# Other instruction prices in the list schedule of a hybrid decoder layer

## The chip, the core and the metric

The kernel runs as one program on one core of a Trainium2 chip. TensorE (PE in the profile; its weight loads are PEld) multiplies matrices into PSUM, VectorE (DVE) and ScalarE (ACT) do elementwise work, GpSimd (POOL) a little, and SyncE (SP) issues the DMAs. The metric is the time of one execution on the device in microseconds (us); less is better.

## What is computed

One layer of a decoder with two kinds of heads. 2128 tokens go through it: 16 meta tokens and 2048 prompt tokens as one sequence, and 8 sample sequences of 8 tokens each. The width is 1024. After an RMS norm one projection gives q, k, v and u:

```python
q, k, v, u = mixer_front(xp, g_mix, w_in, g_q, g_k)
o_att = prompt_window_attention(q, k, v, sinks)        # window 128, 8 query heads, 2 kv heads
o_ssm, hr, hi = ssm_mixer(u, h0, h0, *ssm_p)           # 32 groups, 64 complex states each
xp = mixer_back(xp, o_att, o_ssm, *back_p)

def mixer_back(x, o_att, o_ssm, g_att_out, g_ssm_out, w_out, g_ffn, w_gate, w_up, w_down):
    mix = concat([rms_norm(o_att, g_att_out), rms_norm(o_ssm, g_ssm_out)])
    h = x + mix @ w_out
    f = rms_norm(h, g_ffn)
    return h + (silu(f @ w_gate) * (f @ w_up)) @ w_down
```

The state mixer turns u into 64 complex states a group by a scan over the positions, h = lambda h + B u, reads them out with C, and ends with a GELU and a gate. All inputs and outputs are float32; the inner width of the FFN is 2816.

## The kernel before

**A recorder and a planner.** The kernel's stages don't issue instructions. Every call on an engine is recorded by `Plan.note` (line 225) with its dependencies (read after write, write after read and after write by regions of tiles, and reuse of a buffer), its cost from `Plan.price` (line 316) and its engine. The profile gives line 279, the call in `note`, for nearly all instructions. At the end `Plan.issue` (line 341) lays all recorded instructions in an order, once, by list scheduling: each has a tail, its cost plus the longest chain of costs behind it, with `hop` (line 296) added for each step between two instructions, and a bias for some parts (`BIAS`, line 288: attention 6 us, the state mixer's later steps more and more). The planner keeps a clock for each engine. It goes on with the engine that can start earliest, and there takes the one with the longest tail among those that are ready by then. The eight PSUM banks are given out in the same walk. The instructions are then issued in the order of their planned starts, each on its engine, SP's DMAs among them. So a price never changes an instruction; it changes the place of instructions in the queues of the engines, and which bank a product gets. An engine works its queue off in that order and stands when the next instruction's inputs aren't there.

**Prices before.** ns for n elements per partition: VectorE 1.04 n + 65 (0.52 n for copies and scalar operations from SBUF, 65 more for a scalar operand that is a tile), for the scan and the masked maximum too; ScalarE 0.83 n + 60 or 95, and 90 for each of bias, scale tile and accumulator; TensorE 0.417 n + 3 for products in fp32r, 1.68 n + 3 in fp32, 0.85 per row for a transpose.

**Stages** (by the names of `part`):
- `u` (`phase_u`, line 502): six blocks of tokens. A block's x is split in a high and a low part in fp32r (xh on ScalarE, xl on VectorE), three products per weight tile (`mm3`, line 433) add up pu in PSUM, 96 products of up to 384 columns a block; 1/rms comes from sums over partitions (pb) and a pow on GpSimd; VectorE writes us = pu x 1/rms through a view whose inner step isn't one element. Beside it `aw` splits the qkv weights.
- `prep` (`phase_prep`, line 570): the parameters of the state mixer, on VectorE mostly; they go through DRAM (kD, miD).
- `att` and `ssm` (`mix_step`, line 1201): 17 tiles of 128 tokens for attention and 16 blocks of two groups for the state mixer, recorded side by side. Attention of a tile: 48 products pa in fp32r (q, k, v), qn on VectorE, transposes pt, 16 score products on 64 rows in pairs for the two kv heads (`scores`, line 1032), masked maxima mx on VectorE, exp on ScalarE, transposes of P, then four products P x V with 64 output columns each, in pairs for the two kv heads (`p_v`, line 1099). The state mixer of two groups: product px, rotation on VectorE in products of 64 partitions (xt, xs), two scans (gg), rotation back, hc (`ssm_h`, line 883), product yp of hc (`ssm_y`, line 889), GELU on ScalarE and VectorE (g), gate product px, store to oD. Every second step also makes tables of sine and cosine (f, y, co, si).
- `ow`, `out`, `start`, `norm`, `turn`: output projection (products po), norms and operands of the FFN.
- `ffn` (`phase_ffn`, line 1428): the FFN by a scheme with seven products in place of eight (ga, gb, gc, da, db).

Of the kernel before, what the change touches and what calls it, by code (L numbers as in the profile page):

```python
# [9 lines left out]
F32R = mybir.dt.float32r  # L10
# [160 lines left out]

class Op:
    __slots__ = ("eng", "cost", "wait", "call", "deps", "order", "next", "succ", "tail", "left", "ready", "start", "n", "set", "tiles",
                 "into", "part", "dma", "port")


class Plan:
# [18 lines left out]
    def turn(self, old, *new):  # L196

        pools = [LazyPool(self, *p) for p in new]

        def call():  # L200
            for p in [p for p in reversed(self.open) if p in old]:
                p.ctx.close()
                self.open.remove(p)
            for p in pools:
                p.ctx = ExitStack()
                p.got = p.ctx.enter_context(self.tc.tile_pool(name=p.name, bufs=p.bufs, side=p.side))
                self.open.append(p)

        if not old:
            call()  # L210
            return pools
        g = Op()
        g.eng, g.n, g.cost, g.wait, g.set, g.tiles, g.into = "gate", len(self.ops), 0, 0, None, [], None
        g.part = None
        g.order, g.dma, g.port = set(), False, False
        g.deps = set().union(*[p.ops for p in old])
        for p in old:
            p.over = True
        for p in pools:
            p.gate = g.n  # L220
        g.call = call
        self.ops.append(g)
        return pools

    def note(self, eng, name, args, kw):
        o = Op()
# [7 lines left out]
        deps, order = set(), set()  # L234
# [31 lines left out]
        o.dma = "dma" in name  # L266
        o.cost, o.wait = self.price(eng, name, args, kw)
        o.port = self.ported(eng, name, outs, args, kw)
        fn = args[2] if eng == "scalar" and name == "activation" else None
        o.set = {AF.Sin: "sin", AF.Silu: "silu", AF.Exp: "exp", AF.Tanh: "exp"}.get(fn)  # L270

# [5 lines left out]
        def call():  # L277
# [9 lines left out]

    part, BIAS = None, {"prep": 3e3, "att": 6e3, **{"ssm%d" % i: 2e3 * (i - 4) for i in range(5, 17)}}

    HOP = {("tensor", "scalar"): 200, ("tensor", "vector"): 200, ("tensor", "gpsimd"): 225,  # L290
           ("vector", "tensor"): 256, ("vector", "scalar"): 200, ("vector", "gpsimd"): 205,
           ("scalar", "tensor"): 281, ("scalar", "vector"): 142, ("scalar", "gpsimd"): 170,
           ("gpsimd", "tensor"): 135, ("gpsimd", "vector"): 74, ("gpsimd", "scalar"): 75,
           ("tensor", "tensor"): 0, ("vector", "vector"): 127, ("scalar", "scalar"): 150, ("gpsimd", "gpsimd"): 102}

    def hop(self, a, b):
        if "gate" in (a, b):
# [3 lines left out]
        return 1100 if a == "sync" else self.HOP[a, b]  # L301

    PORT = False

    def ported(self, eng, name, outs, args, kw):

# [9 lines left out]
    def price(self, eng, name, args, kw):  # L316

        psum = lambda v: isinstance(v, Lazy) and v.base.psum
        out = kw.get("out", args[0] if args else None)
        n = int(np.prod(out.shape[1:]))  # L320
        ap = lambda v: isinstance(v, (Lazy, bass.AP))
        if "dma" in name:
            return 100 + out.shape[0] * n * 4 / (370 if out.shape[-1] >= 128 else 190), 1000
        if eng == "tensor":
            if name == "transpose":
                return 0.85 * args[1].shape[0], 0
            return (0.417 * n if args[1].dtype == F32R else 1.68 * max(n, 64)) + 3, 0
        if eng == "scalar":
            c = 0.83 * n + (60 if psum(args[1]) else 95) + 90 * ap(kw.get("bias")) + 90 * ap(kw.get("scale")) + 90 * ("accum_out" in kw)
            return c, 0  # L330
        if eng == "vector":
            if name == "tensor_reduce":
                return 1.04 * int(np.prod(args[1].shape[1:])) + 70, 0
            fast = name in ("tensor_copy", "tensor_scalar", "memset") and not psum(args[1] if len(args) > 1 else None)
            c = 65 + 65 * (name in ("tensor_scalar", "scalar_tensor_tensor") and ap(args[2]))
            return (3 if name == "reciprocal" else 0.52 if fast else 1.04) * n + c, 0
        if kw.get("op") == ALU.pow:
            return 165 * n + 300, 0
        return {"tensor_scalar": 1.37, "memset": 0.8, "tensor_copy": 1.0}.get(name, 2.15) * n + 135, 0

    def issue(self):
# [28 lines left out]
        banks = [(0.0, "b%d" % i) for i in range(8)]  # L370
        whole = {b: False for _, b in banks}
        left = {t: t.count for o in ops for t in o.tiles if t.psum}
        order, table, pipe, port = [], None, 0.0, 0.0
        for _ in ops:
            get = [min((b for b in banks if whole[b[1]] or not y), default=(1e12,)) for y in (False, True)]
            at = lambda o: (max(o.ready, get[o.into.seeded][0], 1e12 * bool(need.get(o.into))) if o.into and "tag" not in o.into.kw
# [3 lines left out]
            o = max((o for o in cand[e] if at(o) <= t), key=lambda o: o.tail)  # L380
# [10 lines left out]
            end = t + o.cost  # L391
            if o.dma:
                pipe = end = max(t + 2000 * (e == "gpsimd"), pipe) + o.cost
            if o.set is not None and o.set != table:
                end += 1283
                table = o.set
            free[e] = t + 1340 if o.dma and e == "gpsimd" else end
            if o.port:
                port = end
# [1378 lines left out]
```

## Time and profile before

| | |
|---|---|
| time, median of 3 runs | 2149.49 us (2148.3 to 2153.83) |
| profiled execution | 2150.36 us, of which its span 2148.5 us |
| TensorE busy | 2049.7 us (95%) |
| VectorE busy | 1735.1 us (81%) |
| ScalarE busy | 1295.8 us (60%) |
| mean granted clock of TensorE | 0.977 |

The span runs from the first to the last instruction. By the products in the trace the stage of u ends near 130 us, the mixers near 560, the output projection near 775, and the rest is the FFN. "Busy" is the union of an engine's instructions; a product in fp32 has two records, one in fp32r has one. The granted clock is 1.00 at 2.4 GHz; a mean below that over a stretch says that part of it ran at 1.2 GHz.

### The profile page before, as it was taken

The page shows a single profiled execution, that of the slowest core. Times are in us where ns is not written, and L with a number is a line of the kernel's source. Part 1 is how long each engine was busy: PE and PEld are TensorE (multiplying, and loading weights), DVE is VectorE, ACT ScalarE, POOL GpSimd, SP SyncE. Part 2 cuts the span into 40 slices and gives each one's busy share as a digit, 9 for nine tenths or more (in the row PEclk, how much of TensorE's full clock was granted, in tenths as well). Part 3 has the DMA queues.
Part 4 walks back from the last instruction along what each step waited for, and adds up shares of the span by engine and source line. Part 5 has one row for each costly group of instructions (what it writes and reads, how often), then busy time and mean ns, then how long its engine had stood idle before and what let it go on. Part 6 is the DMA issues. An engine that isn't in the chain of part 4 may idle for free.

```text
span 2148.5 us, 35113 instructions
## 1 busy us (share of the span) xinstructions
PE 2049.7 (95%) x12625; PEld 1938.0 (90%) x12625; DVE 1735.1 (81%) x3688; ACT 1295.8 (60%) x2831; POOL 101.6 (5%) x97
## 2 busy tenths in 40 slices
PE   7989988898999999999999999999999999999998
PEld 7977766665898999999999899999999999999997
DVE  8776999987488769878788888878877987877876
ACT  6335766657444437566566756656656775665665
POOL 2001120112011000000000000000000000000000
PEclk9899999998899999999999999999999999999999
DMA  6673332224343645323322553332322722222222
GB/s 224 151 145 77 80 86 74 69 73 126 93 122 90 181 150 176 104 76 112 105 80 79 174 160 103 116 94 81 115 70 99 243 87 89 79 69 88 81 70 87
DMA packets 195150, 235.05 MB, mean 109 GB/s; under 512 B 54000, under 2 KB 155792, under 8 KB 194832
## 3 DMA queue, kind: packets, MB, share of 16 engines
q1 hardware_dynamic: 194976, 232.81, 36.3%
q8 instruction: 99, 1.62, 0.3%
q14 instruction: 75, 0.61, 0.1%
HBM read 187.92 MB, written 45.83 MB: 109 GB/s over the span
## 4 chain that ended last, share of the span: by engine, by line
PE 77%; DVE 14%; ACT 4%; DMA 3%; issue 1%; POOL 1%; SPq 0%; DVEq 0%; ACTq 0%
PE ga L279 23%; PE gc L279 12%; PE db L279 11%; PE da L279 8%; PE po L279 7%; PE gb L279 6%; PE pa L279 3%; PE pu L279 2%; PE ps L279 2%; DVE xs L279 2%; DVE xt L279 1%; DVE P L279 1%; PE pt L279 1%; PE yp L279 1%; ACT wb L279 1%
## 5 line engine op out<-in xcount | busy, mean ns | idle before, releaser
L279 PE MATMUL ga<-X,wb 128*128 128x352 f32 x3168 | 721.0, 324 | 7.0 <-ACT acc L279 2.9
L279 PEld LDWEIGHTS ga<-X,wb 128*128 128x128 f32 x3168 | 544.0, 188 | 10.9 <-ACT gb L279 3.8
L279 PE MATMUL gc<-X,wb 128*128 128x352 f32 x1584 | 401.6, 323 | 2.4 <-ACT acc L279 1.4
L279 PEld LDWEIGHTS gc<-X,wb 128*128 128x128 f32 x1584 | 278.7, 188 | 3.6 <-ACT acc L279 2.3
L279 ACT ACTIVATE wb<-S 128x512 fp32r<-128x512 f32 (+1 forms) x306 | 187.4, 617 | 154.3 <-PE ga L279 74.3
L279 DVE TENSOR_TENSOR wb<-S,wb 128x512 fp32r<-128x512 f32 (+1 forms) x306 | 203.5, 670 | 57.9 <-ACT wb L279 26.7
L279 ACT ACTIVATE wb<-r 128x512 fp32r<-128x512 f32 (+1 forms) x242 | 146.9, 613 | 124.9 <-PE gc L279 46.2
L279 PE MATMUL gb<-X,wb 128*128 128x352 f32 x792 | 216.7, 323 | 0.0
L279 PE MATMUL da<-wb 128*128 128x352 f32 x936 | 208.9, 323 | 3.2 <-DVE acc L279 1.6
L279 DVE TENSOR_TENSOR wb<-r,wb 128x512 fp32r<-128x512 f32 (+1 forms) x242 | 159.9, 668 | 51.6 <-PE gb L279 22.3
L279 PE MATMUL db<-wb 128*128 128x352 f32 x792 | 162.9, 323 | 4.4 <-ACT db L279 4.4
L279 PEld LDWEIGHTS da<-wb 128*128 128x128 f32 x936 | 159.4, 188 | 5.5 <-ACT wb L279 4.6
L279 PE MATMUL db<-gb,wb 128*128 128x352 f32 x792 | 161.0, 323 | 0.0
L279 ACT ACTIVATE wb<-fr 128x512 fp32r<-128x512 f32 (+1 forms) x166 | 101.9, 619 | 92.0 <-PE gc L279 40.1
L279 PE MATMUL pa<-wb,xh 128*128 128x512 f32 (+3 forms) x544 | 143.8, 357 | 0.3 <-DVE qn L279 0.3
L279 DVE TENSOR_TENSOR wb<-fr,wb 128x512 fp32r<-128x512 f32 (+1 forms) x166 | 110.8, 674 | 39.3 <-PE gb L279 16.0
L279 PEld LDWEIGHTS gb<-X,wb 128*128 128x128 f32 x792 | 142.2, 188 | 0.0
L279 PEld LDWEIGHTS db<-wb 128*128 128x128 f32 x792 | 132.7, 188 | 6.0 <-ACT db L279 6.0
L279 PEld LDWEIGHTS db<-gb,wb 128*128 128x128 f32 x792 | 133.1, 188 | 0.3 <-ACT db L279 0.3
L279 ACT ACTIVATE acc<-db 128x352 f32<-128x352 f32 x288 | 119.5, 457 | 20.7 <-PE db L279 19.9
L279 PE MATMUL po<-oh,wb 128*128 128x352 f32 x576 | 121.8, 335 | 2.1 <-ACT oh L279 1.5
L279 ACT ACTIVATE db<-acc 128x352 f32<-128x352 f32 x276 | 120.5, 465 | 2.4 <-DVE ru L279 2.2
(257 smaller groups left out, 3746.8 us busy)
## 6 DMA issues: line engine op xcount, KB each, us to landing
r<-w_up SPq DMA_DIRECT2D x41, 512.0 KB
r<-w_gate SPq DMA_DIRECT2D x38, 512.0 KB
r<-w_down SPq DMA_DIRECT2D x34, 512.0 KB
fr<-w_gate SPq DMA_DIRECT2D x28, 512.0 KB
fr<-w_down SPq DMA_DIRECT2D x26, 512.0 KB
fr<-w_up SPq DMA_DIRECT2D x25, 512.0 KB
acc<-xT SPq DMA_DIRECT2D x6, 1408.0 KB
hD<-acc SPq DMA_DIRECT2D x6, 1408.0 KB
```

The source lines that it names most:

```text
L279: getattr(getattr(self.nc, eng), name)(*[f(v) for v in args], **{k: f(v) for k, v in kw.items()})
```

## The change

Three things change in the planner. The hops between engines get other values for six of the pairs. The price of an instruction depends on its part: for parts outside `DENSE` (the output projection, its weights, norms and the FFN) a product in fp32r costs 11 ns more, and elementwise operands whose innermost step isn't one element cost more per element. For all parts, 64-partition VectorE work costs 100 ns more, the scan 2.1 n + 60, the masked maximum 1.08 n + 75, VectorE's rate is 1.05 in place of 1.04, and products in fp32 cost half where they use 64 rows or 64 columns of the array, and 3 ns more of fixed cost. Last, the planner adds 95 ns after a product whose geometry (64 rows, 64 columns, full) differs from that of the product planned before it. No instruction is added, removed or changed; their order and the banks may change.

```diff
--- before.py
+++ after.py
@@ -171,7 +171,7 @@
 
 class Op:
     __slots__ = ("eng", "cost", "wait", "call", "deps", "order", "next", "succ", "tail", "left", "ready", "start", "n", "set", "tiles",
-                 "into", "part", "dma", "port")
+                 "into", "part", "dma", "port", "geo")
 
 
 class Plan:
@@ -212,7 +212,7 @@
         g = Op()
         g.eng, g.n, g.cost, g.wait, g.set, g.tiles, g.into = "gate", len(self.ops), 0, 0, None, [], None
         g.part = None
-        g.order, g.dma, g.port = set(), False, False
+        g.order, g.dma, g.port, g.geo = set(), False, False, None
         g.deps = set().union(*[p.ops for p in old])
         for p in old:
             p.over = True
@@ -266,6 +266,7 @@
         o.dma = "dma" in name
         o.cost, o.wait = self.price(eng, name, args, kw)
         o.port = self.ported(eng, name, outs, args, kw)
+        o.geo = self.geometry(args) if eng == "tensor" else None
         fn = args[2] if eng == "scalar" and name == "activation" else None
         o.set = {AF.Sin: "sin", AF.Silu: "silu", AF.Exp: "exp", AF.Tanh: "exp"}.get(fn)
 
@@ -287,11 +288,11 @@
 
     part, BIAS = None, {"prep": 3e3, "att": 6e3, **{"ssm%d" % i: 2e3 * (i - 4) for i in range(5, 17)}}
 
-    HOP = {("tensor", "scalar"): 200, ("tensor", "vector"): 200, ("tensor", "gpsimd"): 225,
-           ("vector", "tensor"): 256, ("vector", "scalar"): 200, ("vector", "gpsimd"): 205,
-           ("scalar", "tensor"): 281, ("scalar", "vector"): 142, ("scalar", "gpsimd"): 170,
+    HOP = {("tensor", "scalar"): 200, ("tensor", "vector"): 200, ("tensor", "gpsimd"): 275,
+           ("vector", "tensor"): 256, ("vector", "scalar"): 118, ("vector", "gpsimd"): 165,
+           ("scalar", "tensor"): 281, ("scalar", "vector"): 142, ("scalar", "gpsimd"): 180,
            ("gpsimd", "tensor"): 135, ("gpsimd", "vector"): 74, ("gpsimd", "scalar"): 75,
-           ("tensor", "tensor"): 0, ("vector", "vector"): 127, ("scalar", "scalar"): 150, ("gpsimd", "gpsimd"): 102}
+           ("tensor", "tensor"): 0, ("vector", "vector"): 119, ("scalar", "scalar"): 133, ("gpsimd", "gpsimd"): 102}
 
     def hop(self, a, b):
         if "gate" in (a, b):
@@ -301,6 +302,14 @@
         return 1100 if a == "sync" else self.HOP[a, b]
 
     PORT = False
+    DENSE = "out", "start", "norm", "turn", "ffn", "ow"
+
+    def geometry(self, args):
+
+        out, a = args[0], args[1]
+        rows = a.shape[0]
+        c = a.shape[1] if len(a.shape) > 1 else 1
+        return "rows" if rows == 64 else "cols" if out.shape[0] == 64 and c == 64 else "full"
 
     def ported(self, eng, name, outs, args, kw):
 
@@ -324,16 +333,25 @@
         if eng == "tensor":
             if name == "transpose":
                 return 0.85 * args[1].shape[0], 0
-            return (0.417 * n if args[1].dtype == F32R else 1.68 * max(n, 64)) + 3, 0
+            if args[1].dtype == F32R:
+                return 0.417 * n + (3 if self.part in self.DENSE else 14), 0
+            return 1.68 * max(n, 64) * (0.5 if self.geometry(args) != "full" else 1) + 6, 0
+
+        slow = self.part not in self.DENSE and sum(isinstance(v, Lazy) and v.shape[-1] > 1 and v.idx.strides[-1] not in (0, v.idx.itemsize)
+                   for v in list(args) + list(kw.values()))
         if eng == "scalar":
-            c = 0.83 * n + (60 if psum(args[1]) else 95) + 90 * ap(kw.get("bias")) + 90 * ap(kw.get("scale")) + 90 * ("accum_out" in kw)
+            c = (0.83 + 1.08 * bool(slow) * (name == "activation")) * n + (60 if psum(args[1]) else 95) + 90 * ap(kw.get("bias")) + 90 * ap(kw.get("scale")) + 90 * ("accum_out" in kw)
             return c, 0
         if eng == "vector":
             if name == "tensor_reduce":
                 return 1.04 * int(np.prod(args[1].shape[1:])) + 70, 0
             fast = name in ("tensor_copy", "tensor_scalar", "memset") and not psum(args[1] if len(args) > 1 else None)
-            c = 65 + 65 * (name in ("tensor_scalar", "scalar_tensor_tensor") and ap(args[2]))
-            return (3 if name == "reciprocal" else 0.52 if fast else 1.04) * n + c, 0
+            c = 65 + 100 * (out.shape[0] == 64) + 65 * (name in ("tensor_scalar", "scalar_tensor_tensor") and ap(args[2]))
+            if name == "tensor_tensor_scan":
+                return 2.1 * n + 60, 0
+            if name == "tensor_tensor_reduce":
+                return 1.08 * n + 75, 0
+            return ((3 if name == "reciprocal" else 0.52 if fast else 1.05) + 0.75 * (slow > 0)) * n + c, 0
         if kw.get("op") == ALU.pow:
             return 165 * n + 300, 0
         return {"tensor_scalar": 1.37, "memset": 0.8, "tensor_copy": 1.0}.get(name, 2.15) * n + 135, 0
@@ -370,7 +388,7 @@
         banks = [(0.0, "b%d" % i) for i in range(8)]
         whole = {b: False for _, b in banks}
         left = {t: t.count for o in ops for t in o.tiles if t.psum}
-        order, table, pipe, port = [], None, 0.0, 0.0
+        order, table, pipe, port, geo = [], None, 0.0, 0.0, None
         for _ in ops:
             get = [min((b for b in banks if whole[b[1]] or not y), default=(1e12,)) for y in (False, True)]
             at = lambda o: (max(o.ready, get[o.into.seeded][0], 1e12 * bool(need.get(o.into))) if o.into and "tag" not in o.into.kw
@@ -394,6 +412,9 @@
             if o.set is not None and o.set != table:
                 end += 1283
                 table = o.set
+            if o.geo != geo and o.geo:
+                end += 95
+                geo = o.geo
             free[e] = t + 1340 if o.dma and e == "gpsimd" else end
             if o.port:
                 port = end
```

## Rows read from the trace of the kernel before

**Rows 1.** The page: busy us of each engine, its share of the span, and instructions.
```profile
PE 2049.7 (95%) x12625; PEld 1938.0 (90%) x12625; DVE 1735.1 (81%) x3688; ACT 1295.8 (60%) x2831; POOL 101.6 (5%) x97
```

**Rows 2.** Busy us by stage: stretch, length, engines, then PEclk, DMA share, GB/s.
```profile
0.00:130.00 130.00, 115.33 (x668) 111.47 (x669) 105.47 (x270) 63.08 (x110) 17.68 (x12) 0.91 0.69 188
130.00:170.00 40.00, 31.07 (x168) 26.98 (x166) 33.55 (x67) 13.44 (x18) 5.06 (x6) 0.88 0.68 131
170.00:240.00 70.00, 68.89 (x483) 54.14 (x483) 45.55 (x163) 48.22 (x127) 8.91 (x11) 0.99 0.27 68
240.00:450.00 210.00, 186.62 (x1060) 136.84 (x1060) 198.39 (x526) 139.21 (x321) 32.12 (x39) 0.97 0.29 80
450.00:510.00 60.00, 55.22 (x318) 39.88 (x316) 46.96 (x140) 28.10 (x82) 7.18 (x7) 0.97 0.19 55
510.00:560.00 50.00, 38.17 (x268) 29.45 (x267) 38.43 (x117) 42.06 (x111) 10.57 (x8) 0.76 0.45 120
560.00:775.00 215.00, 206.62 (x1320) 201.28 (x1320) 141.40 (x295) 83.21 (x154) 18.80 (x14) 0.97 0.42 125
775.00:2148.00 1373.00, 1347.74 (x8353) 1337.96 (x8351) 1125.39 (x2115) 878.43 (x1912) 1.26 (x1) 1.00 0.34 108
```

**Rows 3.** Waits of PE, 0 to 560 us: total us, times, longest.
```profile
PE yp L279 <- DVE hc L279: 10.0, 5, 2.7
...
PE pt L279 <- DVE qn L279: 6.5, 3, 3.4
...
PE px L279 <- DVE g L279: 4.0, 5, 1.1
PE ps L279 <- DVE mx L279: 3.4, 3, 2.2
...
PE yp L279 <- DVE mx L279: 2.0, 2, 1.6
```

**Rows 4.** Timeline of VectorE, then of PE, around one stall: start, us, instruction.
```profile
332.69 1.22 DVE L279 TENSOR_TENSOR xl<-r,xh 128x1024 fp32r<-128x1024 f32 x1
333.83 0.69 DVE L279 TENSOR_TENSOR hc<-xt,xs 128x514 f32<-128x514 f32 x1
...
334.57 2.10 PE L279 MATMUL yp<-hc,mo 128*128 128x266 f32 x4 [2.02 <-DVE hc L279]
...
352.05 1.17 PE L279 MATMUL yp<-hc,mo 128*128 128x266 f32 x4
```

**Rows 5.** Two stretches of 10 us, columns as in rows 2.
```profile
10.00:20.00 10.00, 10.00 (x57) 9.74 (x56) 8.54 (x34) 5.42 (x8) 7.78 (x2) 1.00 1.01 348
330.00:340.00 10.00, 7.45 (x41) 5.47 (x41) 9.49 (x23) 4.52 (x10) 3.02 (x4) 0.83 0.30 79
```

**Rows 6.** VectorE by shape, 0 to 560 us: busy us, mean ns | idle before.
```profile
L279 DVE TENSOR_TENSOR xs<-px,si 64x258 f32<-64x258 f32 x64 | 27.1, 424 | 1.0
L279 DVE TENSOR_TENSOR xs<-gg,si 64x516 f32<-64x516 f32 x32 | 22.4, 700 | 0.4
L279 DVE TENSOR_TENSOR_SCAN gg<-mag,xt 128x258 f32<-128x258 f32 x32 | 21.0, 693 | 0.0
...
L279 DVE TENSOR_TENSOR us<-pu,rb 128x384 f32<-128x384 f32 x16 | 12.6, 870 | 1.4 <-ACT rb L279 1.4
```

**Rows 7.** Timeline of PE: runs of 64-row and 64-column products, and what follows.
```profile
182.49 2.06 PE L279 MATMUL ps<-kT,qT 64*128 64x128 f32 x32
184.47 0.66 PE L279 MATMUL pt<-idt,se 128*128 128x128 f32 x4
...
194.28 1.94 PE L279 MATMUL ps<-PT,v 128*64 128x512 f32 x8
196.15 0.66 PE L279 MATMUL pt<-idt,qn 128*128 128x128 f32 x4
...
409.81 1.07 PE L279 MATMUL ps<-PT,v 128*64 128x512 f32 x2
410.82 1.17 PE L279 MATMUL yp<-u,it 128*128 128x266 f32 x4
```

## Prediction

> **What bounds the kernel now.** The change touches only the costs with which the planner orders the work, so the question is where a better or worse order can move the end. I read the busy times first: TensorE is busy for 95% of the span and VectorE for 81% [rows 1]. The table by stage splits that [rows 2]. In the output projection and the FFN (560 to 2148 us) TensorE idles 8.4 + 25.3 us of 1588; VectorE has room. Ahead of 560 us the picture is another: the stage of u (0 to 130) leaves TensorE idle 14.7 us and VectorE 24.5; at 130 to 170 they idle 8.9 and 6.5. From 170 to 240 TensorE idles 1.1 and VectorE 24.5; from 240 to 450 it turns over, TensorE idles 23.4 and VectorE 11.6 (198.4 busy of 210); from 450 to 510 they idle 4.8 and 13.0. So the mixers have two bounds that take turns, and the reader should see that neither engine is full over the whole: from 170 to 510 TensorE works 310.7 of 340 us and VectorE 290.9. Everything from 560 on is one dense TensorE stream that starts when the mixers are through, so what is won or lost ahead of 560 us moves the end by as much.
>
> Then the waits of TensorE ahead of 560 us [rows 3]: products of the mixers wait 10.0 us in 5 places for hc, the last VectorE step of the state scan, 6.5 for qn, 4.0 for g and 3.4 + 2.0 for the score maxima: 25.9 us. One of these in close-up [rows 4]: yp waits 2.02 us for hc, which VectorE starts at 333.83, after an xl of 1.22 us. The clock granted over those ten microseconds is 0.83 against 1.00 in dense stretches, which of the two levels means some time at 1.2 GHz [rows 5]: behind the stall four records of yp last 2.10 us, at the 2.4 GHz level later 1.17 [rows 4]. So such a stall costs about 0.9 us more on that one item.
>
> **The change part by part.** Every number of microseconds that follows for a price is worked out from the formula in the diff; the measured one has its rows.
>
> *VectorE prices.* A 64-partition product of 258 columns goes from 1.04x258+65 = 333 to 1.05x258+165 = 436 ns; the trace has 424. The one of 516 goes from 602 to 707; measured 700. The scan goes from 333 to 602; measured 693 [rows 6]. A block of two groups has 4, 2 and 2 of them: 4x0.103 + 2x0.105 + 2x0.269 = 1.16 us more of planned VectorE work, some 19 us over 16 blocks. The product that writes us (384 columns) goes from 464 to 756; measured 870 [rows 6].
>
> *TensorE prices.* The 64-row products of the scores go from 218 to 113.5 ns. 16 of them (32 records) run in 184.47 - 182.49 = 1.98 us, 124 ns each [rows 7]. The 64-column products P x V go from 863 to 436; four run in 196.15 - 194.28 = 1.87 us, 468 each [rows 7]. A product in fp32r gets 11 ns more: 384 columns were 163 and become 174, and in the stage of u 57 records fill 10 us, 175 each [rows 5]. Per tile of 128 tokens: 16x(-0.1045) + 4x(-0.427) + 48x0.011 = -2.85 us; each change between the three geometries adds 0.095; two score calls and P x V, entered and left, make six, with some splits about ten (an estimate), 0.95. Net some -1.9 us a tile, -30 us over 16.
>
> So in the plan the balance of the mixers moves by some 3 us a tile from TensorE to VectorE, to where the trace has it. The old plan believed that hc, qn, g and the maxima come early and put their readers early in TensorE's order; an engine that issues in order then stands while the qkv products (pa) behind the reader would be ready. With the longer VectorE prices these readers fall behind some pa work. That is the gain: of 25.9 us I take half, **-13 us**. Not more, because in 240 to 450 VectorE itself has only 11.6 us to give, and a stall that is filled there partly becomes a wait of VectorE; not less, because the longer scan also lengthens the tail of px (its matmul), so that TensorE feeds VectorE earlier at 170 to 240, where VectorE idles 24.5 us behind 68.9 us of TensorE work [rows 2]. The bounds of this term are 0 and -29.3 (TensorE's whole idle time, 170 to 510).
>
> *The clock.* Fewer stalls of 2 us keep the clock: five hc stalls at 0.9 us each, half of them gone, **-2 us** (0 to -8.8, which is the missing clock from 170 to 510: 0.01x70 + 0.03x210 + 0.03x60).
>
> *What stays too cheap.* An unpaired 64-column product costs more than its price: alone it takes 410.82 - 409.81 = 1.01 us where the paired one takes 0.47 and the new price is 0.436 [rows 7]. The planner sees no pairs. Where it splits some more than now, I charge **+2 us** (0 to +20, the last in the third rival).
>
> *Stage of u and parameters.* 576 fp32r products get 11 ns and 24 us products some 0.2 to 0.3 us in the plan. The old plan was wrong there by 7% on one engine, so the sequence around them may move; TensorE idles 14.7 us there. I take **+1 us** (-5 to +5): the parameter chain feeds kD and the first mixer steps, and nothing in its own prices changes.
>
> *End of the mixers, 510 to 560.* TensorE idles 11.8 us at a clock of 0.76 [rows 2]. DMAs, table loads and the pow on GpSimd keep their prices; the new hops are shorter by 82 ns at most. **0** (-4 to +4). All DMAs leave SP's queue in planned order, so each that moves is moved with its neighbours; the wait for the last store of the mixers stands in this stretch and stays.
>
> *Later stages.* Only hops, 0.01 ns per column of VectorE and 3 ns per small fp32 product move; they can still swap neighbours. TensorE idles 8.4 + 25.3 us there in all, at the seams mostly. **0** (-5 to +5): a seam that is laid out anew costs or gives back what one costs now.
>
> Sum: -13 - 2 + 2 + 1 = **-12 us**. The profiled execution took 2150.4 us (span 2148.5 and 1.9 around it), 0.9 above the median of 2149.5; 2149.5 - 12 gives **2138 us**, 0.5% faster.
>
> **What the skill says.** The Trainium skill, TensorE: Matmul & The Clock Gate, section Part 3: Packing small matmuls, says that products on different row or column groups of the array run at the same time. The trace agrees for neighbours (124 ns per score product, 468 per P x V product) and shows what the rule costs where a partner is missing (1.01 us) [rows 7]; a price of one half holds for pairs alone, which speaks against this change and makes the third rival. The Trainium skill, Perfetto Trace Analysis, section Identifying the Most-Contended Engine, calls matmul busy time a poor measure and takes the share of weight loads, while VectorE's occupancy is fair. By that rule 240 to 450 (136.8 us of weight loads, 198.4 of VectorE [rows 2]) is a VectorE stretch; that is the second rival.
>
> **Rivals.** *First, deeper:* the plan with VectorE as its long engine feeds it from 170 on and nearly all stalls go: -25.9 of waits, -7 of clock and +2 for broken pairs, 2119 us. For it: both engines together idle 29.3 and 49.1 us in 170 to 510. Against it: a greedy planner looks one instruction ahead, and hc hangs on a serial chain.
>
> *Second, no change:* VectorE bounds 240 to 450 and its work is not shortened by a nanosecond. A filled TensorE stall there returns as a later stall; only the 11.6 us of VectorE idle are to be had, a third of them 4, and the later stages or the stage of u take 2 of these back: 2147 us. For it: VectorE is busy 94% there.
>
> *Third, slower:* the halved prices make the planner scatter 64-column and 64-row products among other work, since it sorts by tails and not by partners. Now ten runs of P x V hold all four products of a tile ([rows 7] has one of them); if all 40 of these lose their partner, each costs 1.01 - 0.47 = 0.54 us, together +21 us of TensorE work, which counts in full only where TensorE bounds. With 60% of it on the path, +13, and no stall removed, 2162 us. It decides from the point where more than half of the pairs that stand now are split. For it: the charge of 95 ns for a changed geometry is under what a split costs, and is not looked at when the next instruction is chosen. Against it: both halves of a pair become ready together.
>
> **How the numbers follow.** Under 0.3% (6.4 us) a difference can't be told from none with this kernel. Forecast 0.45 (2138), deeper gain 0.12 (2119), no change 0.20 (2147), slower 0.23 (2162). So faster 0.57, same 0.20, slower 0.23. The range goes from 2116 (the first rival and 3 us of the small terms) to 2162 (the third); beyond each end lies about 1 in 10. The forecast's own range is 2128 to 2143.
>
> **What would show it.** Right: TensorE's waits for hc, qn, g and mx ahead of 560 us fall from 25.9 to about 13 us; its first dense stretch of po products begins some 12 us earlier than 560; the clock from 240 to 450 rises above 0.97; VectorE's idle time from 170 to 240 shrinks. From the start of the po products to the end the span keeps its length within 5 us. Wrong: the same waits under other names (hc gone, px or yp waiting for xs in its place) with VectorE at 95% and more; runs of P x V products of two records in place of eight; a later part longer by over 5 us, which would put the hops on the path.

## The result and the profile after

The changed kernel takes 2122.6 us (2116.86 to 2124.06, 4 runs), the kernel before beside it 2149.46: a ratio of 0.9866 with an interval of 0.9843 to 0.989, 26.9 us less. That is faster, as forecast, and more than twice the forecast 12 us; the first rival (2119 us, given 0.12) came nearest.

The page of the profiled execution (2123.75 us), its span and its first part, busy us and share:

```profile
span 2122.0 us, 35096 instructions
...
PE 2044.9 (96%) x12625; PEld 1933.6 (91%) x12625; DVE 1731.3 (82%) x3688; ACT 1291.3 (61%) x2829; POOL 107.1 (5%) x97
```

Busy time by stage of the kernel after, to be laid beside [rows 2] (stretch, length, PE, PEld, DVE, ACT, POOL, PEclk, DMA share, GB/s):

```profile
0.00:130.00 130.00, 115.21 (x676) 111.88 (x677) 100.75 (x260) 61.44 (x108) 17.72 (x12) 0.92 0.74 188
130.00:170.00 40.00, 32.08 (x173) 26.76 (x171) 32.45 (x66) 14.65 (x21) 3.38 (x7) 0.96 0.67 125
170.00:240.00 70.00, 65.71 (x385) 48.62 (x383) 65.33 (x188) 46.80 (x115) 12.82 (x12) 0.98 0.36 100
240.00:450.00 210.00, 198.91 (x1178) 147.14 (x1176) 194.68 (x546) 139.75 (x339) 33.02 (x38) 0.99 0.27 71
450.00:510.00 60.00, 55.28 (x385) 40.90 (x383) 43.76 (x138) 39.71 (x111) 9.95 (x7) 1.00 0.42 113
510.00:560.00 50.00, 45.91 (x308) 40.21 (x309) 31.14 (x98) 27.53 (x79) 8.83 (x6) 0.83 0.36 106
560.00:775.00 215.00, 206.54 (x1317) 202.07 (x1316) 154.66 (x317) 89.53 (x164) 20.11 (x14) 0.97 0.43 129
775.00:2148.00 1373.00, 1325.30 (x8222) 1315.98 (x8220) 1108.51 (x2084) 871.91 (x1895) 1.26 (x1) 1.00 0.34 105
```

The reader should see 170 to 240 us first: VectorE goes from 45.55 busy to 65.33. From 240 to 450 it works about as much as before (194.7), and TensorE works 12.3 us more in it (198.9 for 186.6). The granted clock of 240 to 450 goes from 0.97 to 0.99, that of 450 to 510 from 0.97 to 1.00.

Up to its first po product (557.8 us before, 535.3 after) TensorE has nearly the same work to do in both (2949 and 2940 records). The kernel before, then after:

```profile
0.00:557.80 557.80, 493.12 (x2949) 396.55 (x2949) 467.90 (x1275) 332.31 (x759) 81.52 (x82) 0.93 0.42 109
0.00:535.30 535.30, 488.40 (x2940) 391.41 (x2940) 459.18 (x1268) 324.25 (x755) 84.50 (x81) 0.96 0.44 112
```

It idles 46.9 us instead of 64.7 and is busy 4.7 us less, at a clock of 0.96 instead of 0.93: 17.8 + 4.7 are the 22.5 us by which the po products start earlier.

The waits of TensorE from 0 to 560 us, to be laid beside [rows 3] (total us, times, longest):

```profile
PE pt L280 <- ACT P L280: 7.8, 19, 3.9
...
PE yp L280 <- issue: 4.9, 1, 4.9
PE px L280 <- DVE g L280: 2.8, 4, 1.1
...
PE ps L280 <- DVE mx L280: 2.2, 2, 1.2
...
PE pa L280 <- DVE qn L280: 1.9, 3, 1.3
...
PE yp L280 <- DVE hc L280: 0.7, 2, 0.5
...
PE pt L280 <- DVE qn L280: 0.6, 2, 0.3
```

hc fell from 10.0 to 0.7, the five rows of [rows 3] together from 25.9 to 6.3. Others grew: P (exp on ScalarE) from 4.6 to 7.8, and there is one new wait of 4.9 us of a yp for which no releaser is seen.

Where the time went is read best from a few products by tile: record counts, durations (least, median, most), first and last start. The kernel before, then after:

```profile
L279 PE MATMUL pu<-xl,wuh x192: 278/334/689, 8.5 to 146.9; 128*128 128x384 f32 x128, 128*128 128x256 f32 x32, 128*128 128x336 f32 x32
...
L279 PE MATMUL pa<-wb,xh x544: 274/388/793, 129.5 to 514.9; 128*128 128x256 f32 x86, 128*128 128x512 f32 x85, 128*80 128x512 f32 x6, 128*80 128x256 f32 x5
...
L279 PE MATMUL yp<-hc,mo x64: 385/388/768, 203.0 to 500.1; 128*128 128x266 f32 x64
```

```profile
L280 PE MATMUL pu<-xl,wuh x192: 277/334/689, 8.2 to 136.7; 128*128 128x384 f32 x128, 128*128 128x256 f32 x32, 128*128 128x336 f32 x32
...
L280 PE MATMUL pa<-wb,xh x544: 274/388/776, 137.3 to 498.9; 128*128 128x512 f32 x87, 128*128 128x256 f32 x84, 128*80 128x512 f32 x6, 128*80 128x256 f32 x5
...
L280 PE MATMUL yp<-hc,mo x64: 385/387/649, 163.6 to 476.6; 128*128 128x266 f32 x64
```

The last pu of this row starts 10 us earlier, the first yp of hc 39 us earlier, the last one 23.5. The first po product starts at 535.3 instead of 557.8, the first ga product of the FFN at 757.7 instead of 778.4 (20.7 less), and from there to the end it takes 1364.3 us instead of 1370.1 (5.8 less). 20.7 + 5.8 are the 26.5 us between the two spans. From the first po product to the end it is 1586.7 us instead of 1590.7, 4.0 less.

### The profile page after: what moved, and what is told of

It reads as the page before. It is cut to its first block, busy times and chain, and to the rows that moved or that the text cites. A ratio compares the mean times of both kernels' runs of the same rounds, so it can differ in the third digit from the quotient of the medians.

```text
span 2122.0 us, 35096 instructions
## 1 busy us (share of the span) xinstructions
PE 2044.9 (96%) x12625; PEld 1933.6 (91%) x12625; DVE 1731.3 (82%) x3688; ACT 1291.3 (61%) x2829; POOL 107.1 (5%) x97
## 4 chain that ended last, share of the span: by engine, by line
PE 80%; DVE 10%; ACT 4%; DMA 3%; issue 2%; POOL 1%; SPq 0%; DVEq 0%; ACTq 0%; POOLq 0%
PE ga L280 24%; PE gc L280 12%; PE db L280 11%; PE da L280 8%; PE po L280 7%; PE gb L280 6%; PE pa L280 3%; PE ps L280 3%; PE pu L280 2%; ACT P L280 1%; PE pt L280 1%; PE px L280 1%; DVE xs L280 1%; DVE P L280 1%; DVE acc L280 1%
## 5 line engine op out<-in xcount | busy, mean ns | idle before, releaser
L280 PE MATMUL ga<-X,wb 128*128 128x352 f32 x3168 | 733.8, 323 | 3.8 <-ACT q L280 1.5
L280 PE MATMUL gc<-X,wb 128*128 128x352 f32 x1584 | 413.7, 323 | 1.5 <-ACT acc L280 1.5
L280 PE MATMUL pa<-wb,xh 128*128 128x256 f32 (+3 forms) x544 | 146.2, 358 | 2.7 <-DVE qn L280 1.9
L280 DVE TENSOR_TENSOR wb<-fr,wb 128x512 fp32r<-128x512 f32 (+1 forms) x166 | 111.3, 675 | 35.0 <-PE gb L280 12.3
```

Source lines behind the costliest of these rows:

```text
L280: getattr(getattr(self.nc, eng), name)(*[f(v) for v in args], **{k: f(v) for k, v in kw.items()})
```

## The experiments

The first ga product parts the time well, since the output projection overlaps the mixers' end by different amounts; "FFN" is the time from it to the end of the span, "first yp" the first product that reads hc. These three times are from one profile each, and the whole time of one kernel spreads by 1.6 to 13.4 us over its runs, so a few us between two of them say little. Ratios with their 95% intervals are against the kernel before on the same chip.

| kernel | ratio | first yp | first ga | FFN |
|---|---|---|---|---|
| before | 1 | 203.0 | 778.4 | 1370.1 |
| after | 0.9866 (0.9843 to 0.989) | 163.6 | 757.7 | 1364.3 |
| oldlater | 0.9879 (0.9863 to 0.9896) | 157.1 | 759.4 | 1368.7 |
| newlater | 0.9988 (0.9979 to 0.9998) | 204.2 | 783.2 | 1363.7 |
| oldtails | 0.9895 (0.9878 to 0.9912) | 203.5 | 767.7 | 1362.5 |
| newtails | 0.9971 (0.9956 to 0.9986) | 157.4 | 776.0 | 1369.7 |
| vector | 0.9979 (0.9967 to 0.9992) | 197.8 | 779.9 | 1367.5 |
| tensor | 0.9877 (0.9851 to 0.9903) | 157.6 | 755.8 | 1369.2 |
| noswitch | 0.9925 (0.9896 to 0.9953) | 162.3 | 766.0 | 1363.3 |
| oldu | 0.9807 (0.9782 to 0.9831) | 161.8 | 744.2 | 1363.5 |
| half | 0.9852 (0.9835 to 0.9869) | 161.1 | 750.6 | 1369.3 |
| fp14 | 0.9982 (0.9971 to 0.9992) | 205.4 | 779.6 | 1368.9 |
| switch85 | 0.9855 (0.9836 to 0.9875) | 160.8 | 760.0 | 1366.5 |
| bias4 | 1.0009 (0.9999 to 1.002) | 197.4 | 782.9 | 1368.6 |
| halfpv | 0.99 (0.9883 to 0.9917) | 167.5 | 761.0 | 1367.2 |
| halfscores | 1.0006 (0.9994 to 1.0019) | 198.0 | 788.5 | 1369.2 |
| halfclock | 0.9961 (0.9945 to 0.9978) | 203.6 | 775.4 | 1367.3 |
| halftail | 0.993 (0.9915 to 0.9944) | 157.7 | 766.8 | 1368.9 |
| oldpu | 0.9873 (0.9854 to 0.9892) | 159.4 | 756.2 | 1364.6 |
| halfhops | 0.9831 (0.9815 to 0.9848) | 157.8 | 746.4 | 1364.5 |

**Which engine's prices.** My theory: VectorE's true length places the readers of its results later. Rival: TensorE's lighter work does it. *vector* keeps only the new prices of VectorE and ScalarE, *tensor* only those of TensorE and the 95 ns.

```diff
 vector: in price(), TensorE branch
-            if args[1].dtype == F32R:
-                return 0.417 * n + (3 if self.part in self.DENSE else 14), 0
-            return 1.68 * max(n, 64) * (0.5 if self.geometry(args) != "full" else 1) + 6, 0
+            return (0.417 * n if args[1].dtype == F32R else 1.68 * max(n, 64)) + 3, 0
 and without the 95 ns, with the old HOP
```

> Only the prices of VectorE and ScalarE are new; TensorE's prices, hops and geometry as before. If the gain comes from the true length of VectorE's work (19 us more of it in the plan), most of it stays: 2130 us or less, hc waits under 3 us. If it comes from the lighter TensorE (30 us less in the plan), it is near 2145.

```diff
 tensor: in price(), VectorE branch (the scan, the masked maximum and the stepped operands likewise), with the old HOP
-            c = 65 + 100 * (out.shape[0] == 64) + 65 * (name in ("tensor_scalar", "scalar_tensor_tensor") and ap(args[2]))
+            c = 65 + 65 * (name in ("tensor_scalar", "scalar_tensor_tensor") and ap(args[2]))
```

> Only TensorE's prices and the 95 ns are new; VectorE, ScalarE and hops as before. VectorE theory: 2140 to 2150 us with hc waits of 7 us or more. TensorE theory (a plan in which TensorE has room takes the mixers' products early): 2130 or less.

*tensor* gives 0.9877, *vector* 0.9979. My theory falls: the prices that it was built on are worth 0.2% alone, and the change gives as much without them. The windows of *vector*, 170 to 240 and 240 to 450 us, show a VectorE that is fed earlier there too (59.2 us busy, then 200.6), yet its first ga product comes at 779.9 us, no earlier than before:

```profile
170.00:240.00 70.00, 66.77 (x438) 51.76 (x438) 59.22 (x182) 48.78 (x127) 10.86 (x12) 0.96 0.29 79
240.00:450.00 210.00, 194.48 (x1175) 148.47 (x1176) 200.64 (x560) 135.29 (x327) 33.23 (x39) 0.98 0.29 79
```

**Which of TensorE's prices.** *half* is the kernel before with the half price alone, *fp14* the kernel before with 11 ns more for a product in fp32r outside the later parts.

```diff
 half
-            return (0.417 * n if args[1].dtype == F32R else 1.68 * max(n, 64)) + 3, 0
+            if args[1].dtype == F32R:
+                return 0.417 * n + 3, 0
+            return 1.68 * max(n, 64) * (0.5 if self.geometry(args) != "full" else 1) + 3, 0
 fp14
+                return 0.417 * n + (3 if self.part in self.DENSE else 14), 0
+            return 1.68 * max(n, 64) + 3, 0
```

> The kernel before with one new price: products in fp32 on 64 rows or 64 columns cost half. No 95 ns, no 11 ns, old hops, old VectorE. TensorE's prices together took 22.6 us off the time to the first ga product. If the half price is the one that does it, by the shorter chains of attention, the first yp comes near 160 us and the time is 2135 us or less; if the plan then only believes too much room, some 2145 to 2155.

> The kernel before with one new price: a product in fp32r outside the later parts costs 11 ns more. If the gain is in the true pace of the products that fill TensorE (pu 174 and pa 228 ns), 2140 us or less, with the first yp still near 200 us; if it is in the half price, 2147 to 2153.

*half* gives 0.9852, all that the whole change gives; *fp14* 0.9982. The same windows of *half*, and its wait for hc:

```profile
170.00:240.00 70.00, 69.24 (x416) 52.51 (x414) 66.11 (x187) 49.16 (x127) 9.98 (x12) 1.00 0.30 81
240.00:450.00 210.00, 195.78 (x1170) 144.85 (x1168) 198.00 (x550) 140.17 (x332) 32.64 (x38) 0.98 0.27 75
```

```profile
PE yp L280 <- DVE hc L280: 0.5, 1, 0.5
```

VectorE is at 66.1 us from 170 to 240, hc has gone from 10.0 to 0.5, and no price of VectorE was touched. *halfpv* and *halfscores* halve the one kind of product or the other:

```diff
 halfpv
-(0.5 if self.geometry(args) != "full" else 1)
+(0.5 if self.geometry(args) == "cols" else 1)
 halfscores
+(0.5 if self.geometry(args) == "rows" else 1)
```

> The kernel before, half price for the 64-column products P x V alone (68 of them in the plan, 863 to 431 ns each, 29 us). If these long products are what blocked TensorE's planned clock, most of the gain: 2130 us or less. If the scores are, 2143 or more.

> The kernel before, half price for the 64-row score products alone (some 270 of them, 218 to 109 ns, 29 us in the plan as well). If both kinds count by their microseconds, the two runs are alike, near 2135 us each. If it is the long P x V, 2143 or more.

P x V alone gives 0.99, two thirds of it; the scores alone nothing (1.0006), and what they add to the rest (0.9852 against 0.99) they add only beside P x V. The two take the same 29 us out of the planned work of TensorE, so these microseconds are not what counts; what does is told under rank below.

**Clocks or tails.** The planner uses a price twice: in its clocks, for when an engine and an input are there, and in the tails, for who goes first. *oldtails* and *newtails* part the whole change so, *halfclock* and *halftail* the half price.

```diff
 oldtails / halfclock: tails from the old (full) price, clocks from the new (half) one
-            o.tail = o.cost + o.wait + ...
+            o.tail = o.tcost + o.wait + ...
 newtails / halftail: the other way round
```

> The planner's clocks (when an engine is free, when an input is there, the 95 ns) take the new prices and hops; the tails, by which it picks among the ready, take the old ones. If the gain ahead of 560 us comes from readers that are placed when their inputs are really there (the step of my forecast), it stays: some 2125 to 2130 us, waits for hc still near 1 us. If it comes from the longer tails of the state mixer's products, by which VectorE is fed earlier, the first yp goes back from 164 to near 200 us and the time to 2140 or more.

> The mirror: tails from the new prices and hops, clocks from the old ones without the 95 ns. Placement theory: near 2145 to 2150 us with hc waits near 10 us. Tail theory: VectorE is busier from 170 to 240 us (65 in place of 46), the first yp near 164 us and the time near 2130.

> The half price of both kinds in the planner's clocks alone; the tails keep the full price. The placement theory (readers land where their inputs are there) asks for most of the gain here, 2130 us or less, even with the first yp near 200 us. The rank theory asks for 2143 or more.

> The half price of both kinds in the tails alone; the clocks keep the full price. Rank theory: 2130 us or less, first yp near 160 us. Placement theory: first yp may be early, but waits for hc stay near 8 to 10 us and the time is 2143 or more.

To the first ga product the whole change gives 20.7 us, new clocks alone 10.7, new tails alone 2.4; the half price gives 27.8 us, in the clocks alone 3.0, in the tails alone 11.6. Either way the two together give more than their sum. With new clocks and old tails the wait for hc is gone altogether (*oldtails* has none). What each does is seen in the same rows by tile. *halftail* and its wait for hc:

```profile
L284 PE MATMUL pu<-xl,wuh x192: 278/334/522, 8.1 to 133.0; 128*128 128x384 f32 x128, 128*128 128x256 f32 x32, 128*128 128x336 f32 x32
...
L284 PE MATMUL pa<-wb,xh x544: 276/388/793, 133.6 to 504.4; 128*128 128x256 f32 x86, 128*128 128x512 f32 x85, 128*80 128x512 f32 x6, 128*80 128x256 f32 x5
...
L284 PE MATMUL yp<-hc,mo x64: 385/388/813, 157.7 to 471.3; 128*128 128x266 f32 x64
```

```profile
PE yp L284 <- DVE hc L284: 6.6, 9, 1.6
```

*halfclock* and its wait for hc:

```profile
L284 PE MATMUL pu<-xl,wuh x192: 278/334/525, 8.0 to 145.1; 128*128 128x384 f32 x128, 128*128 128x256 f32 x32, 128*128 128x336 f32 x32
...
L284 PE MATMUL pa<-wb,xh x544: 274/388/776, 127.9 to 515.3; 128*128 128x256 f32 x86, 128*128 128x512 f32 x85, 128*80 128x512 f32 x6, 128*80 128x256 f32 x5
...
L284 PE MATMUL yp<-hc,mo x64: 385/388/652, 203.6 to 507.3; 128*128 128x266 f32 x64
```

```profile
PE yp L284 <- DVE hc L284: 3.3, 4, 1.8
```

With the half price in the tails the first pa product starts at 133.6, after the last pu (133.0 in this row; pu<-xh,wul, the last of the three kinds of pu, ends the stage 0.5 us later). Without it pa starts at 127.9 and the last block of u is drawn out to 145.1 by attention's products among it. So it is in the kernel before (pa from 129.5, pu to 146.9, in its rows by tile above). Counted to the last pu of all three kinds, the twenty kernels fall into two groups: in eleven pa starts after the last pu and the first yp comes at 157 to 164 us; in eight pa starts 16 to 21 us ahead of the last pu and the first yp comes at 197 to 205; *halfpv* stands between (11.5 us ahead, 167.5). This is the switch that I had not seen: attention's products outranked the last products of u, and the whole state mixer, VectorE's work, waits for those. For the half price, the tails alone leave hc waits of 6.6 us in 9 places and the clocks alone 3.3 in 4; the two together leave 0.5 (*half*).

The switch doesn't decide the time by itself. *oldtails* hasn't thrown it and has its first ga product at 767.7; *newtails* has, and has it at 776.0:

```profile
170.00:240.00 70.00, 63.76 (x390) 47.05 (x389) 69.47 (x200) 46.84 (x112) 7.92 (x11) 1.00 0.32 87
240.00:450.00 210.00, 188.53 (x1112) 141.05 (x1110) 183.80 (x515) 137.47 (x334) 32.67 (x38) 0.95 0.25 68
```

In *newtails* VectorE is fed from 170 on, more than in the changed kernel, but then idles 26.2 us from 240 to 450, while TensorE waits 7.7 us for hc. How much of an early start is kept hangs on the clocks too: of the kernels with old clocks and new tails *newtails* keeps 2.4 us of it and *halftail* 11.6.

**Is it rank alone?** *bias4* changes the rank of attention without any price.

```diff
-{"prep": 3e3, "att": 6e3, ...
+{"prep": 3e3, "att": 4e3, ...
```

> The kernel before with the bias of the attention parts at 4 in place of 6 us and no new price. Half prices shorten attention's chain of score and P x V products by some 2 us a tile, so if the earlier first yp is a matter of rank between attention and the state mixer alone, this run has it near 160 us too, VectorE busy 60 us or more from 170 to 240, and a time like that of the new tails alone, 2143 to 2150. If the true clocks are what counts, the same time; a time under 2135 would say that the rank alone does it.

1.0009, and pa still begins ahead of the last pu:

```profile
L279 PE MATMUL pu<-xl,wuh x192: 277/334/522, 8.1 to 141.4; 128*128 128x384 f32 x128, 128*128 128x256 f32 x32, 128*128 128x336 f32 x32
...
L279 PE MATMUL pa<-wb,xh x544: 274/388/1006, 125.5 to 516.5; 128*128 128x512 f32 x88, 128*128 128x256 f32 x83, 128*80 128x512 f32 x6, 128*80 128x256 f32 x5
...
L279 PE MATMUL yp<-hc,mo x64: 385/389/652, 197.4 to 500.3; 128*128 128x266 f32 x64
```

2 us less of rank don't throw the switch. The tails themselves say why. They are times of the plan, worked out by running the planner's code of each kernel, and not times of the chip: the first pa product, and the last block of u from its first pu to its last.

| kernel | first pa | last block of u |
|---|---|---|
| before | 899.7 | 896.3 to 893.1 |
| bias4 | 897.7 | 896.3 to 893.1 |
| halfscores | 892.2 | 888.8 to 885.5 |
| halfpv | 879.4 | 880.4 to 876.2 |
| half | 871.9 | 880.4 to 876.2 |

The longer tail goes first. So attention leads in the first three, stands among the last block in *halfpv* and behind it in *half*, as in their traces. The P x V products of a tile stand one behind the other in the chain of attention, and what is halved there adds up along the tail of an early tile: P x V takes 20.3 us off it and the scores 7.5, though both take 29 us out of the planned work. The same numbers say why the first yp moves by 39 us and the last pu by only 10: the first px product of the state mixer has a tail of 868.5 in all five. Before, the first pa products of four tiles of attention rank ahead of it (899.7, 893.8, 884.8 and 875.9); with the half price that of one tile does (871.9). A larger bias was not tried.

**The 95 ns.** *noswitch* takes them out of the changed kernel, *switch85* takes 10 of them.

```diff
 noswitch
-            if o.geo != geo and o.geo:
-                end += 95
-                geo = o.geo
 switch85
-                end += 95
+                end += 85
```

> The changed kernel without the 95 ns for a changed geometry; the half prices stay. If the charge only makes TensorE's clock in the plan truer (about 1 us a tile), a loss of 0 to 4 us: 2122 to 2127. If it is what keeps pairs together, runs of P x V with all four products get fewer and the time goes up by more than 6 us.

> The changed kernel with 85 ns for a changed geometry in place of 95. No theory says that 10 ns of the plan matter in themselves (127 changes, 1.3 us of planned time). If times move with prices smoothly, 2122 to 2124 us. If the order is chaotic in small prices, it can land anywhere some 10 us around 2122.6, and single prices explain less than they seem to.

85 in place of 95 is the same time (0.9855). Without them 0.9925: 9 runs of P x V hold all four products, with them 11 (10 before). But *half* has no such charge either, has 8 such runs, and is as fast as the changed kernel, so pairing isn't what the 0.6% is; which interplay it is stays open.

**The stage of u.** *oldu* takes the 11 ns of a product in fp32r and the charge for stepped operands (those whose innermost step isn't one element) away from the parts u, prep and aw; *oldpu* takes away the 11 ns alone.

```diff
 oldu
-    DENSE = "out", "start", "norm", "turn", "ffn", "ow"
+    DENSE = "out", "start", "norm", "turn", "ffn", "ow", "u", "prep", "aw", None
 oldpu
-(3 if self.part in self.DENSE else 14)
+(3 if self.part in self.DENSE + ("u", "prep", "aw", None) else 14)
```

> The changed kernel with the parts u, prep and aw priced like the later parts (3 ns in place of 14 for a product in fp32r, no extra for stepped operands). The last product of the stage of u moved from 147.6 to 137.1 us. If its own prices did that, it goes back to about 147 and the time to some 2130; if the mixers' prices did it (they pull px ahead), it stays within 3 us of 2122.6.

> The changed kernel with 3 ns in place of 14 for the fp32r products of the parts u, prep and aw; the us writes keep the new price. If the 11 ns on pu cost what the run with all old prices in u got back, some 2109 us; if the us writes' price does, 2122; if neither alone does, the order there is a matter of chance and the time is between.

*oldu* is the fastest kernel of the study, 2108.95 us, 0.9807: the measured prices of the stage of u cost the change some 13 us. The products are not it (*oldpu* 0.9873), so it is the dearer us writes, the only work of these parts with a stepped operand, alone or with the products. The gain isn't in the stage of u, which ends at 135.0 us in place of 137.1; it is at the mixers' end, where the last pa starts at 486.0 in place of 499.1. Why a price in the first stage moves the last is open.

**The later stages.** *oldlater* is the changed kernel with all later parts at old prices and hops, *newlater* the kernel before with all later parts at new ones.

```diff
 oldlater
-        o.cost, o.wait = self.price(eng, name, args, kw)
+        o.cost, o.wait = (self.price0 if self.part in self.DENSE else self.price)(eng, name, args, kw)
 and hop0 in place of hop, in tails and clocks, behind an instruction of such a part; newlater the other way round
```

> The changed kernel, but the instructions of the output projection and the FFN are planned with all the old prices and hops. If the 5.8 us that the FFN got shorter come from its own new hops and rates, this run takes some 2122.6 + 5.8 = 2128 us, with the FFN (first ga product to the end) back at 1370 us. If they come from the state in which the earlier stages hand over, it stays at 2122.6 and the FFN at 1364.

> The kernel before, but the output projection and the FFN are planned with the new prices and hops; everything ahead of them keeps the old ones. Own hops theory: 2149.5 - 5.8 = 2143.7 us, FFN 1364 us, first po product still near 558 us. Handover theory: 2149.5 us, FFN 1370.

The FFN takes 1368.7 and 1363.7 us: it follows its own prices and hops, whatever came ahead. Over all twenty profiles here it takes 1362.5 to 1366.5 us in the eight with the new hops in the later parts' clocks (mean 1364.1) and 1367.2 to 1370.1 in the twelve with the old (mean 1368.7). In *newlater* the stages ahead of it give most of that back (0.9988). *halfhops* joins the half price and the new hops:

```diff
 halfhops: half, and
-           ("vector", "tensor"): 256, ("vector", "scalar"): 200, ("vector", "gpsimd"): 205,
+           ("vector", "tensor"): 256, ("vector", "scalar"): 118, ("vector", "gpsimd"): 165,
 and the other changed hops
```

> The kernel before with the half price and the new hops and nothing else. In seven profiles the FFN took 1362.5 to 1366.5 us with the new hops and 1367.5 to 1370.1 without. If that adds to the half price: 2122.9 - 5 = 2118 us, FFN near 1364. If the new hops spoil the mixers' order, 2123 or more with the FFN still near 1364.

2116.33 us, 0.9831, FFN 1364.5: the hops are what counts there, the two add, and these two edits give at least as much as the whole change (0.9866; the intervals just overlap). Of the 5.8 us between the kernels before and after, 4.6 come from two stretches of the FFN, where TensorE waits for operands of ScalarE and VectorE: before they leave it idle for 8.1 and 4.4 us,

```profile
1200.00:1320.00 120.00, 111.86 (x673) 109.08 (x673) 109.08 (x218) 85.66 (x198) 0.00 (x0) 0.99 0.55 178
1660.00:1760.00 100.00, 95.61 (x587) 93.75 (x587) 92.42 (x187) 75.18 (x174) 0.00 (x0) 1.00 0.57 182
```

and after for 4.9 and 3.0:

```profile
1179.30:1299.30 120.00, 115.11 (x707) 112.94 (x706) 111.31 (x222) 89.19 (x204) 0.00 (x0) 1.00 0.56 177
1639.30:1739.30 100.00, 97.00 (x596) 95.19 (x595) 92.74 (x186) 74.51 (x172) 0.00 (x0) 1.00 0.53 167
```

## Why the prediction was right and wrong

Against the 12 us of the forecast stand the 26.5 us between the two spans. TensorE's idle time ahead of the first po product fell by 17.8 us (forecast 13) and its busy time there, with the clock, by 4.7 (2); from the first po product on it is 4.0 us less (0). The 2 + 1 us charged for unpaired products and the stage of u lie within the 22.5.

**What bounds the kernel:** right. The mixers have two bounds in turn, and what was won ahead of the first ga product moved the end in full.

**The main term, -13 us, failed**, more in its cause than in its size. Its step was that longer VectorE prices push the readers of hc, qn, g and mx behind pa work. But VectorE's prices alone give 0.2% (*vector* 0.9979), and the half price alone gives it all, P x V above all (*half* 0.9852, *halfpv* 0.99). I had counted the half price as 3.4 us a tile off the plan and looked at where TensorE's clock in the plan then stands; I didn't ask what it does to attention's tails against the last products of u, though [rows 2] shows a VectorE that idles behind a full TensorE, which is a matter of who goes first. The longer tail of px, my reason for "not less", is there in the plan of *vector* (877.5 for 868.5), but attention's first pa leads it by 23.8 us even so (901.3). VectorE's idle time from 170 to 240 did shrink, by 19.8 us (45.55 to 65.33 busy), but filling it isn't the gain either: *newtails* fills it too (69.47) and gains 2.4 us to the first ga product. Of the sentence that the readers "fall behind some pa work" the effect was right (the five waits fell to 6.3 us, I said 13), and it needs the clocks: *oldtails*, where it shows without the new rank, has 10.7 us to the first ga product. Which of the prices in its clocks does that wasn't split further; the half price in the clocks alone gives 3.0.

**The clock, -2 us:** too small by its own measure. The missing clock from 170 to 510 went from 8.8 us to 0.02x70 + 0.01x210 = 3.5, and the busy time ahead of the first po product fell by 4.7.

**Unpaired products, +2 us, and the third rival:** didn't come in the changed kernel; the full runs of P x V are 11 for 10. In *halftail*, which has no charge of 95 ns, the pairs did part (2 full runs for 10), with a ratio of 0.993 all the same: a gain and no loss.

**Stage of u, +1 us:** wrong. It ended 10 us earlier, not by its own prices but since attention's products no longer stand among its last ones (*half*: pu to 136.2 with the stage's prices untouched). That is order and not time won: TensorE is busy for 146.4 us of the first 170 before and for 147.3 after. Its own prices cost some 13 us later on (*oldu*), beyond the bound of 5.

**End of the mixers, 0:** right, if counted from the last yp to the first po product: 57.7 us before, 58.7 after.

**Later stages, 0 with a bound of 5:** from the first po product to the end they gave 4.0 us, inside the bound, but the FFN's part of that is -5.8 us, and it is real (4.6 us between the means). The reason for 0 was that a seam laid out anew may cost as well as give; the runs show that it gave in eight of eight.

**The rivals.** *No change* is ruled out by the ratio. *Deeper* had the time and the feature (VectorE fed from 170 on), and should have had more than 0.12: what spoke against it, that hc hangs on a serial chain, holds for one step of two groups, not for when the first step starts. That its 2119 us came near is in part luck: VectorE as the long engine of the plan wasn't the cause, and 5.8 of the 26.5 us come from the FFN, for which it has nothing. *Slower* is ruled out as well.

## What to carry to other kernels

In a list schedule a price acts twice, in the clocks and in the rank. Here a change of rank at a seam between stages (attention's products among the last ones of the stage that feeds the other engine) started the second engine earlier, and truer clocks kept the first one from standing for it; either alone gave 2.4 to 11.6 us to the first ga product, both together 20.7 and 27.8. So ask of each changed price whose tail gets shorter, against whom, and put the two tails side by side: the planner gives them without a run. Look for the stretch in which the second engine idles behind a full first one. And try the edits one by one: two of them (half price and hops) gave at least as much as the whole set of truer prices, and the set without its prices for the stage of u gave more (*oldu* 0.9807).

## What was not expected of the hardware

VectorE takes as long for 258 columns of a product on 128 partitions as on 64 (424 ns [rows 6]; the kernel before, from 0 to 560 us, busy us, mean ns | idle before):

```profile
L279 DVE TENSOR_TENSOR xt<-px,co 128x258 f32<-128x258 f32 x32 | 13.6, 424 | 3.3 <-PE px L279 3.1
```

So most of the 100 ns that the change adds for 64 partitions is missing for this product on 128 as well, where it doesn't add them: its price there is 336 ns.
